# A decoder trunk's first k-tile in four transfers of 128 KB, and the first two tiles' terms alone at the beginning

## The chip, the core and the metric

The kernel runs on one core of a Trainium2 chip. The metric is the device time of one execution in microseconds (us), the median of several runs. A profile is one further execution, recorded by the hardware; its times are in us from the start of its span.

## The reference

Two layers of a causal decoder on 256 tokens of width 1024. Each layer has an attention and an MLP with squared ReLU, each followed by a layer norm of `alpha * x + f(x)`. Only its first product matters here: `x @ w_qkv` of the first attention (16 heads of 64), whose q and k columns are rotated and scored.

```
qkv = (x @ w_qkv).reshape(B, S, 3, H, dh)
q = apply_rotary(qkv[:, :, 0], cos, sin) * (dh ** -0.5)
k = apply_rotary(qkv[:, :, 1], cos, sin)
...
h = layer_norm(DEEPNORM_ALPHA * h + mix, ln_mix_g[i], ln_mix_b[i])
h = layer_norm(DEEPNORM_ALPHA * h + sq_relu_mlp(h, mlp_w_in[i], mlp_w_out[i]), ln_mlp_g[i], ln_mlp_b[i])
```

## The kernel before

**Products in three terms.** Every float32 operand of a large product is split into two fp32r parts, hi (a rounded copy) and lo (the rest), and a product is the sum of hi x hi, hi x lo and lo x hi. `split` (L349) makes them: hi on ScalarE (L351) or, where a part is marked for it, on VectorE as a cast (L353); lo always on VectorE as a subtraction (L356). All matmuls are issued through `mm` (L360).

**The first product.** x transposed stands in HBM beside the first six weight tiles (`NFIRST`), 128 columns each: `xw0` has, for each of eight k-tiles of 128 rows, 256 columns of x and 6 x 128 columns of weights, 1024 float32 columns or 512 KB. One k-tile is one object of the class `Stage` (L379). `STAGE_PARTS` says for k-tile 0, 1, 2 and all later ones how the six weight tiles are cut into parts for the splits, which engine makes each part's hi, and which parts go in one transfer on which queue: part 0 is x, and `(0, 1, "SP")` loads parts 0 to 1 through SP's queue. A part's split waits for the transfer that holds it. In the kernel before, k-tile 0 comes in two transfers: x and tile 0 (192 KB) on SP's queue, tiles 1 to 5 (320 KB) on ACT's. K-tile 1 has x and tiles 0 and 1 on SP's queue, the rest on ACT's; all later loads of the kernel are on SP's queue.

`Stage.mms` (L418) issues one matmul of 256 columns (the tokens) for one weight tile and one of the three terms; six tiles by three terms are the 18 matmuls of a k-tile. They accumulate in three PSUM banks (`acc`), two tiles in each:

```
start, stop = kt == term == j % 2 == 0, kt == KT - 1 and term == 2 and j % 2 == 1
op("PE", 0.12, lambda: mm(ps.t[:, j % 2 * S : j % 2 * S + S], w.t[:, c], xs[kt // 4].t[:, kt % 4, p, :], start, stop),
   [(w, (kt, self.part(j)))] + [(xs[kt // 4], (p, kt, m)) for m in range(2)], [ps])
```

**Fillers.** Ahead of the useful work TensorE runs fillers, matmuls of 512 columns on constants whose result nobody reads (`idle`, L451, one for each entry of `WARM`). One more filler, of 256 columns, stands behind the first useful matmul. In the profile they are written to `tp`, all useful ones of this stage to `acc`.

**What sets the order.** The kernel first collects all operations with estimated costs, then a planner (`Plan.order`) sorts them into one program order by due times, for all engines; buffers are handed out in that order. An engine runs its instructions in this order and waits on semaphores for its inputs. So an edit at one place can move instructions anywhere. DMA issues are instructions of SP or ACT; ACT's first instructions are two DMA issues, then a load of its function table, then the splits.

Of the kernel before, what the change touches and what calls it, by code (L numbers as in the profile page):

```python
# [47 lines left out]
NFIRST = 6  # L48
# [3 lines left out]


STAGE_PARTS = (
    ((1, 3, NFIRST), ("DVE", "ACT", "ACT"), ((0, 1, "SP"), (2, 3, "ACT"))),
    ((2, NFIRST), ("DVE", "ACT"), ((0, 1, "SP"), (2, 2, "ACT"))),
    ((2, NFIRST), ("ACT", "ACT"), ((0, 1, "SP"), (2, 2, "SP"))),
    ((NFIRST,), ("ACT",), ((0, 1, "SP"),)),
)
WARM = (512,) * 8  # L60

# [51 lines left out]
class Plan:  # L115
# [16 lines left out]
    def op(self, eng, cost, fn, reads=(), writes=(), xfer=0.0, early=0.0, ahead=0.0):  # L132
        o = Op()
        o.n, o.eng, o.cost, o.fn, o.xfer = len(self.ops), eng, cost, fn, xfer
        o.early, o.ahead = early, ahead
        o.preds, o.succs, o.bufs = set(), [], set()
        for group, is_write in ((reads, False), (writes, True)):
            for item in group:
                b, key = item if isinstance(item, tuple) else (item, None)
                o.bufs.add(b)  # L140
                for k, st in b.state.items():
                    if key is None or k is None or k == key:
                        if st[0] is not None:
                            o.preds.add(st[0])
                        if is_write:
                            o.preds.update(st[1])
                st = b.state.setdefault(key, [None, []])
                if is_write:
                    if key is None:
                        b.state = {None: [o, []]}  # L150
                    else:
                        st[0], st[1] = o, []
                else:
                    st[1].append(o)
        o.preds.discard(o)
        for p in o.preds:
            p.succs.append(o)
        for b in o.bufs:
            b.left += 1
        self.ops.append(o)  # L160
        return o
# [129 lines left out]
def tile_trunk(  # L291
# [37 lines left out]
    def mk(shape, dt, tag, bufs, space=None):  # L329
        uid[0] += 1  # L330
        return plan.buf(Bufs(space or sb, bufs), shape, dt, tag, bufs, f"{tag}_{uid[0]}")

    def psum(tag):
        return mk([P, 512], F32, tag, 4, ps_pool)
# [24 lines left out]
    def mm(out_ap, lhsT, rhs, start, stop):  # L359
        nc.tensor.matmul(out_ap, lhsT, rhs, start=start, stop=stop)  # L360
# [16 lines left out]
    xs = [mk([P, 4, 2, S], F32R, f"xs{i}", 1) for i in range(2)]  # L377
# [73 lines left out]
    def idle(n, reads=()):  # L451
        ones = nc.const_aps.tensor
        op(
            "PE", n / 2400, lambda: mm(idle_ps.t[:, :n], ones(1.0, [P, P], BF16), ones(1.0, [P, n], BF16), True, True),
            list(reads), [idle_ps],
        )

    for n in WARM:
        idle(n)
# [140 lines left out]

    first_ps = [psum("acc") for _ in range(NFIRST // 2)]
    for st in stages:
        for term in range(3):
            for j in range(NFIRST):
                st.mms(first_ps[j // 2], j, term)
                if st.kt == term == j == 0:
                    idle(256, [(st.hi, (0, 1)), (xs[0], (0, 0, 0))])


    turns = {"score": 0, "prob": 0}  # L610
# [680 lines left out]
```

## Time and profile before

| | |
|---|---|
| median of 3 runs | 559.83 us (559.78 to 559.93) |
| the profiled execution | 560.12 us |
| its span, first to last instruction | 558.3 us |
| TensorE busy | 550.3 us of the span, 3236 matmuls |
| VectorE, ScalarE busy | 412.1 us, 302.0 us |
| first useful matmul starts | 4.59 us |

In the profile PE is TensorE's matmul side, PEld its weight loads, DVE VectorE, ACT ScalarE, SP SyncE; SPq and ACTq are the issues of DMAs. A line such as `4.59 0.41 PE L360 MATMUL acc<-xs,whi ... x1 [0.25 <-ACT xs L351]` reads: start, duration, engine, line, operation, output and inputs by tile name, shapes, how many were merged into the row, and the idle time before with what ended it. A row that merges several has the time from the first one's start to the last one's end or their summed busy time, so neighbouring rows overlap. Matmuls are pipelined: the distance of two starts is less than the duration of one.

### The profile page before, as it was taken

What the parts mean: (1) busy time and instruction counts of PE and PEld (TensorE: products, weight loads), DVE (VectorE), ACT (ScalarE), POOL (GpSimd) and SP (SyncE); (2) the same over time, 40 slices, a digit from 0 to 9 for tenths busy, and PEclk for the clock granted to TensorE, in tenths of its full rate; (3) what the DMA queues carried; (4) which work ended last, traced back from release to release, by engine and by line L of the source; (5) the groups of instructions that cost most, each with busy time, mean ns of one, the idle gap of its engine ahead of it and who ended that gap; (6) DMA issues with size and microseconds to landing.
All of it is one profiled execution on the core that took longest, in us unless ns stands there. A gap on an engine that the chain in (4) does not pass through costs nothing.

```text
span 558.3 us, 8586 instructions
## 1 busy us (share of the span) xinstructions
PE 550.3 (99%) x3236; PEld 470.0 (84%) x3236; DVE 412.1 (74%) x726; ACT 302.0 (54%) x491; POOL 8.6 (2%) x13
## 2 busy tenths in 40 slices
PE   9999999999999999999999999999999999999995
PEld 7988888888888888888888889888888888888884
DVE  6799999897584764854879899789848548558446
ACT  6467898257555455455544566556654554555400
POOL 0000000000000000000000000010000000000001
PEclk9999999999999999999999999999999999999998
DMA  8985246548884754755437535526867456463001
GB/s 333 410 312 190 77 147 220 196 148 300 262 276 145 249 182 154 238 175 191 147 117 265 174 117 164 190 75 196 300 221 262 159 184 225 156 222 114 1 0 75
DMA packets 30136, 105.60 MB, mean 189 GB/s; under 512 B 3344, under 2 KB 4112, under 8 KB 30096
## 3 DMA queue, kind: packets, MB, share of 16 engines
q1 hardware_dynamic: 29808, 104.48, 54.6%
q8 instruction: 25, 0.41, 0.3%
q10 hardware_dynamic: 288, 0.59, 0.3%
q14 instruction: 15, 0.12, 0.1%
HBM read 104.01 MB, written 1.05 MB: 188 GB/s over the span
## 4 chain that ended last, share of the span: by engine, by line
PE 98%; DMA 1%; DVE 0%; POOLq 0%; DVEq 0%; ACT 0%; issue 0%
PE acc L360 59%; PE tp L360 36%; PE tp L689 3%; DMA raw<-in_xw_dram 1%; POOLq L1285 0%; DVE tok L556 0%; DVEq L1285 0%; DVE bst L823 0%; ACT xs L351 0%; DVE mv L801 0%; DVE rstd L802 0%; POOLq L804 0%
## 5 line engine op out<-in xcount | busy, mean ns | idle before, releaser
L356 DVE TENSOR_TENSOR wlo<-raw,whi 128x1024 fp32r<-128x1024 f32 (+3 forms) x186 | 218.2, 1192 | 100.4 <-PE tp L360 47.2
L351 ACT ACTIVATE whi<-raw 128x1024 fp32r<-128x1024 f32 (+1 forms) x184 | 189.0, 1042 | 113.5 <-PE acc L360 68.2
L360 PE MATMUL acc<-whi,ahi 128*128 128x512 f32 (+1 forms) x312 | 121.6, 390 | 0.0
L360 PE MATMUL acc<-wlo,ahi 128*128 128x512 f32 (+1 forms) x312 | 121.0, 388 | 0.0
L360 PE MATMUL tp<-xs,whi 128*128 128x512 f32 x448 | 104.6, 390 | 0.0
L360 PE MATMUL acc<-whi,alo 128*128 128x512 f32 (+1 forms) x312 | 102.7, 387 | 0.0
L360 PEld LDWEIGHTS tp<-xs,whi 128*128 128x128 f32 x448 | 84.0, 188 | 17.3
L360 PEld LDWEIGHTS acc<-whi,alo 128*128 128x128 f32 x312 | 58.6, 188 | 12.1
L360 PEld LDWEIGHTS acc<-whi,ahi 128*128 128x128 f32 x312 | 58.7, 188 | 11.5 <-issue 0.3
L360 PEld LDWEIGHTS acc<-wlo,ahi 128*128 128x128 f32 x312 | 58.7, 188 | 11.2
L360 PE MATMUL acc<-xs,whi 128*128 128x512 f32 (+1 forms) x272 | 56.8, 356 | 0.2 <-ACT xs L351 0.2
L360 PEld LDWEIGHTS tp<-xs,wlo 128*128 128x128 f32 x448 | 55.6, 192 | 1.1
L360 PE MATMUL tp<-xs,wlo 128*128 128x256 f32 x448 | 55.9, 283 | 0.0
L360 PEld LDWEIGHTS acc<-xs,whi 128*128 128x128 f32 x272 | 44.4, 189 | 8.0 <-ACT xs L351 1.2
L351 ACT ACTIVATE ahi<-ta 128x256 fp32r<-128x256 f32 x56 | 23.5, 419 | 44.5 <-DVE ta L556 44.3
L912 ACT ACTIVATE ta<-tp 128x256 f32<-128x256 f32 x56 | 21.3, 380 | 26.2 <-PE tp L360 26.2
L549 DVE TENSOR_TENSOR ta<-tp,ta 128x256 f32<-128x256 f32 x56 | 23.4, 419 | 12.7 <-ACT ta L912 12.6
L360 PE MATMUL acc<-xs,wlo 128*128 128x256 f32 x224 | 30.4, 283 | 0.0
L360 PEld LDWEIGHTS acc<-xs,wlo 128*128 128x128 f32 x224 | 29.1, 191 | 0.9
L360 PE MATMUL acc<-whi,xs 128*128 128x512 f32 (+1 forms) x112 | 29.1, 367 | 0.0
L360 PE MATMUL tp<-whi,xs 128*128 128x512 f32 x80 | 25.2, 396 | 0.0
L556 DVE SCALAR_TENSOR_TENSOR ta<-ta 128x256 f32<-128x256 f32 x56 | 23.8, 425 | 1.8
(102 smaller groups left out, 464.2 us busy)
## 6 DMA issues: line engine op xcount, KB each, us to landing
raw<-in_win_dram SPq DMA_DIRECT2D x64, 512.0 KB, 4.1
raw<-in_wout_dram SPq DMA_DIRECT2D x64, 512.0 KB, 3.9
raw<-in_wqk_dram SPq DMA_DIRECT2D x22, 512.0 KB, 5.5
raw<-in_wo_dram SPq DMA_DIRECT2D x14, 512.0 KB, 3.8
raw<-in_wv_dram SPq DMA_DIRECT2D x8, 512.0 KB, 5.4
g<-in_lng_dram SPq DMA_DIRECT2D x4, 512.0 KB, 7.0
b<-in_lnb_dram SPq DMA_DIRECT2D x4, 512.0 KB, 6.9
raw<-in_wv1a_dram SPq DMA_DIRECT2D x4, 512.0 KB, 3.9
```

Of the source, the lines that this page charges most:

```text
L351: op("ACT", act(n, sbuf=sbuf), lambda: nc.scalar.activation(hi(), src(), AF.Copy), r, whi)
L356: lambda: nc.vector.tensor_tensor(lo(), src(), f32(hi()), op=ALU.subtract), list(r) + list(whi), wlo,
L360: nc.tensor.matmul(out_ap, lhsT, rhs, start=start, stop=stop)
L549: op("DVE", dve(n) + extra, lambda: nc.vector.tensor_tensor(out_ap(), a(), b(), op=alu), r, w)
L556: lambda: nc.vector.scalar_tensor_tensor(dst(), a(), s(), b(), op0=o0, op1=o1), r, w,
L689: nc.tensor.transpose(ps.t[:, c : c + P], src(), ident.t)
L912: op("ACT", act(S), lambda: nc.scalar.activation(u(), ps.t[:, S:], AF.Copy), [ps], uk)
```

## The change

K-tile 0 comes in four transfers of 128 KB: x on SP's queue, tiles 0 and 1 on ACT's, tiles 2 and 3 on SP's, tiles 4 and 5 on ACT's. Its weight tiles are cut into three parts of two tiles (before: one, two and three); the first part's hi is made on VectorE, the others' on ScalarE, as before. Of k-tile 0's matmuls the three terms of tiles 0 and 1 are issued first, then the three terms of the other four; before, the order was by term over all six tiles. The filler among them stands behind the second useful matmul. One of the eight fillers ahead is gone.

```diff
 STAGE_PARTS = (
-    ((1, 3, NFIRST), ("DVE", "ACT", "ACT"), ((0, 1, "SP"), (2, 3, "ACT"))),
+    ((2, 4, NFIRST), ("DVE", "ACT", "ACT"), ((0, 0, "SP"), (1, 1, "ACT"), (2, 2, "SP"), (3, 3, "ACT"))),
     ((2, NFIRST), ("DVE", "ACT"), ((0, 1, "SP"), (2, 2, "ACT"))),
     ((2, NFIRST), ("ACT", "ACT"), ((0, 1, "SP"), (2, 2, "SP"))),
     ((NFIRST,), ("ACT",), ((0, 1, "SP"),)),
 )
-WARM = (512,) * 8
+WARM = (512,) * 7
...
     first_ps = [psum("acc") for _ in range(NFIRST // 2)]
     for st in stages:
-        for term in range(3):
-            for j in range(NFIRST):
-                st.mms(first_ps[j // 2], j, term)
-                if st.kt == term == j == 0:
-                    idle(256, [(st.hi, (0, 1)), (xs[0], (0, 0, 0))])
+
+        n = STAGE_PARTS[0][0][0]
+        todo = sorted((st.kt > 0 or j >= n, term, j) for term in range(3) for j in range(NFIRST))
+        for _, term, j in todo:
+            st.mms(first_ps[j // 2], j, term)
+            if st.kt == term == 0 and j == n - 1:
+                idle(256, [(st.hi, (0, 1)), (xs[0], (0, 0, 0))])
```

Built, the two programs differ only in the first instructions: on TensorE one filler less and the order of k-tile 0's 18 matmuls; on VectorE k-tile 0's cast has 256 columns and not 128, its three weight subtractions 256 each and not 128, 256 and 384, and x's lo stands ahead of all three and not behind the first; on ScalarE the two weight pieces have 256 columns each and not 256 and 384; on SP and ACT one DMA issue more each. From k-tile 1 on, every engine has the same instructions in the same order.

## The prediction

> **What bounds the kernel now.** I read the summary of the page first, then the chain that ended last.
>
> ```profile
> span 558.3 us, 8586 instructions
> ...
> PE 550.3 (99%) x3236; PEld 470.0 (84%) x3236; DVE 412.1 (74%) x726; ACT 302.0 (54%) x491; POOL 8.6 (2%) x13
> ...
> PE 98%; DMA 1%; DVE 0%; POOLq 0%; DVEq 0%; ACT 0%; issue 0%
> ```
>
> TensorE is busy for 550.3 of 558.3 us and carries 98% of the chain. So there are two ways to be faster: fewer TensorE slots, or a stretch in which TensorE has no useful work made shorter. The view of waits, for TensorE alone over the whole span, says where it stood still:
>
> ```profile
> PE tp L360 <- PEq L1276: 0.8, 1, 0.8
> PE acc L360 <- ACT xs L351: 0.2, 1, 0.2
> ```
>
> That is all: it starts at 0.8 us, waits 0.2 us for the first split of x, and then never idles by this view until its work is over. The chain at the beginning, and the timeline (the engines' rows that matter; start, length), show the stretch that the change edits:
>
> ```profile
> 0.73 3.37 DMA raw<-in_xw_dram
> 4.10 0.02 issue
> 4.12 0.42 ACT xs L351
> 4.55 0.04 issue
> 4.59 0.41 PE acc L360
> ...
> 5.13 22.93 PE acc L360 x175
> ```
>
> ```profile
> 0.73 0.89 ACTq L347 DMA_DIRECT2D raw<-in_xw_dram  x2
> 0.73 2.38 SPq L347 DMA_DIRECT2D raw<-in_xw_dram  x5
> ...
> 0.77 3.57 PE L360 MATMUL tp<-const-bfloat16-1.0 128*128 128x512 bf16 x8 [0.77 <-PEq L1276]
> ...
> 1.65 1.28 ACT L351 ACT_TABLE_LOAD   x1 [1.65 <-PEq L1276]
> ...
> 4.45 0.81 ACT L351 ACTIVATE whi<-raw 128x256 fp32r<-128x256 f32 x2
> ...
> 4.59 0.41 PE L360 MATMUL acc<-xs,whi 128*128 128x256 f32 x1 [0.25 <-ACT xs L351]
> 4.59 0.42 DVE L356 TENSOR_TENSOR xs<-raw,xs 128x256 fp32r<-128x256 f32 x1
> ...
> 4.84 0.28 PE L360 MATMUL tp<-const-bfloat16-1.0 128*128 128x256 bf16 x1
> ...
> 4.93 0.92 DVE L356 TENSOR_TENSOR wlo<-raw,whi 128x256 fp32r<-128x256 f32 x2
> 5.65 0.42 ACT L351 ACTIVATE xs<-raw 128x256 fp32r<-128x256 f32 x1 [0.39 <-DMA raw<-in_xw_dram]
> 5.77 0.29 DVE L353 CAST whi<-raw 128x256 fp32r<-128x256 f32 x1
> ...
> 6.10 0.43 DVE L356 TENSOR_TENSOR xs<-raw,xs 128x256 fp32r<-128x256 f32 x1
> ...
> 6.44 1.02 DVE L356 TENSOR_TENSOR wlo<-raw,whi 128x256 fp32r<-128x256 f32 x2
> 6.49 0.88 PE L360 MATMUL acc<-xs,wlo 128*128 128x256 f32 x6
> ...
> 7.21 0.64 PE L360 MATMUL acc<-xs,whi 128*128 128x256 f32 x4
> ```
>
> So the first useful matmul starts at 4.59: the first transfer lands at 4.10, ScalarE splits x in 0.42, and 0.05 goes to the signal. The 18 matmuls of the first k-tile and the small filler last from 4.59 to 7.21, 2.62 us. In steady state one of 256 columns takes a slot of (0.88 - 0.28) / 5 = 0.12, so 19 would take 2.28: some 0.34 is lost to the clock and to waits for ScalarE's second and third piece. All that the change can win lies ahead of 7.21. The order of the rest of every engine's instructions is unchanged.
>
> **The transfers.** Bytes over time (the last two columns are the DMA share and GB/s), then the two queues up to 3 us (q1 is SP's, q10 ACT's), then the first issues with their KB and the time to landing:
>
> ```profile
> 0.00:2.40 2.40, 1.63 (x4) 0.59 (x5) 0.09 (x2) 0.75 (x1) 0.76 (x5) 1.00 0.19 25
> 2.40:3.00 0.60, 0.60 (x3) 0.29 (x2) 0.00 (x0) 0.53 (x1) 0.00 (x0) 1.00 0.87 320
> 3.00:3.40 0.40, 0.40 (x3) 0.13 (x2) 0.00 (x0) 0.00 (x0) 0.00 (x0) 1.00 1.00 393
> 3.40:4.10 0.70, 0.70 (x3) 0.04 (x1) 0.00 (x0) 0.00 (x0) 0.00 (x0) 1.00 1.06 394
> ...
> 5.10:6.00 0.90, 0.90 (x8) 0.78 (x7) 0.90 (x3) 0.51 (x3) 0.00 (x0) 1.00 1.04 266
> 6.00:7.00 1.00, 1.00 (x11) 1.00 (x10) 0.96 (x4) 0.97 (x4) 0.00 (x0) 1.00 1.09 428
> ```
>
> ```profile
> q1 hardware_dynamic: 85, 0.13, 22.9%
> q10 hardware_dynamic: 47, 0.12, 10.1%
> ```
>
> ```profile
> raw<-in_xw_dram ACTq DMA_DIRECT2D x1, 320.0 KB, 3.6
> ...
> raw<-in_xw_dram SPq DMA_DIRECT2D x1, 192.0 KB, 3.4
> ```
>
> Summed up: 0.06 MB by 2.40, 0.25 by 3.00, 0.41 by 3.40, 0.69 by 4.10. By 3.00 the queues have moved 0.13 and 0.12 MB, so both are served side by side at about equal rates. SP's 192 KB (0.197 MB) are through when some 0.39 MB have moved in all, at 3.36; they are signalled at 4.10, a lag of 0.74. After the change x alone is first on SP's queue and two weight tiles on ACT's, 128 KB (0.131 MB) each. Both are through at 0.262 MB, at 3.03, and with the same lag they land at 3.77. Bounds: not at all earlier (4.10), if the lag belongs to the start of the stream and not to its bytes; and 3.65, from the other queue, whose 320 KB end the first k-tile at 0.73 + 3.6 = 4.33: half of that tile's 512 KB, at 394 GB/s, is 0.67 less. I take 3.75, next to the value from x's own queue.
>
> The Trainium skill (DMA: Bandwidth & Descriptors, "Issuing engines are not separate DMA queues") speaks against splitting: transfers issued from several engines run on the same 16 DMA engines and interleave, and only the issue time is saved. The two equal shares above agree; a queue of its own would then bring x nothing, and only the fewer bytes ahead of it count.
>
> Issues: SP and ACT each issue one more. ACT's cost 0.89 / 2 = 0.45, so the table load goes from 1.65 to 2.10 and ends at 3.38, ahead of 3.75: nothing as long as x lands after 3.38. SP's 2.38 / 5 = 0.48 moves its later issues from the second k-tile on; those transfers queue behind a saturated stream (about 390 GB/s), so that is hidden too.
>
> **TensorE's start.** With landing at 3.75 the first useful matmul starts at 3.75 + 0.47 (4.12 to 4.59 now) = 4.22. The groups of the first 8 us have the fillers' mean:
>
> ```profile
> L360 PE MATMUL tp<-const-bfloat16-1.0 128*128 128x512 bf16 x8 | 3.6, 628 | 0.8 <-PEq L1276 0.8
> ```
>
> Dropping one filler: eight end at 4.34, of mean 0.628, so the last starts at 3.71 and they are 0.42 apart; its slot would be over at 4.13, still ahead of 4.22; the seventh's is over at 3.71. The removal is worth 0 here and up to 0.09 with landing at 3.65, and matters only for landing ahead of 3.66. VectorE's first cast grows from one tile to two; the later cast of that size took 0.29, less than ScalarE's 0.42 beside it, so it sets nothing. No split is added: VectorE has a cast and three weight subtractions of 128 to 384 columns now and of 256 then, ScalarE two pieces, 640 columns in all now and 512 then.
>
> **The first k-tile.** The matmul at 4.59 took 0.41 and the filler at 4.84 took 0.28, while this group of equal width took 283 ns in the whole run:
>
> ```profile
> L360 PE MATMUL tp<-xs,wlo 128*128 128x256 f32 x448 | 55.9, 283 | 0.0
> ```
>
> So the clock opens between 4.59 and 4.84, which the granted-clock column does not show. Then, from 4.22: the first matmul's slot 0.25 (4.59 to 4.84), the second 0.21 (half a filler's slot, half its columns), the filler to 4.84; hi x lo of tiles 0 and 1 needs VectorE's lo of x, 4.22 + 0.42 + 0.05 = 4.69, so it starts at 4.84 and ends at 5.08. Their lo parts: VectorE starts them 0.34 after x's lo (4.59 to 4.93), a 256-wide one takes 0.42: 4.22 + 0.34 + 0.42 + 0.05 = 5.03, ready. Two slots, 5.32. The other twelve need ScalarE's two pieces of 256 columns: their transfers complete the 512 KB at some 4.33, and 0.81 gives 5.14 for both. Twelve slots of 0.12: 6.76. Against 7.21 that is 0.45 won: 0.37 from the start, 0.08 from waits that now have other tiles' terms in front.
>
> **The second k-tile.** Its x now stands behind 256 KB on SP's queue, not 192; in equal shares 0.131 MB more in all pass ahead of it, 0.31 us at 428 GB/s, 0.49 at 266. Nothing, if the queues take turns by packets and the longer rows had already had more than their half. So x lands at 5.65, 5.95 or 6.14. TensorE needs its hi at 6.76, its lo at 7.00 and the lo of tiles 0 and 1 at 7.24. VectorE's row: cast at landing + 0.12, x's lo 0.33 later, the next 0.34 later, for 0.42, and 0.05: landing + 1.26. That is 6.91, 7.21 or 7.40: no wait for the first two, 0.16 lost at the last. I take 0.03 lost, near the middle. From the third k-tile on, as many bytes as before stand in front.
>
> **Is it kept to the end?** Later stages:
>
> ```profile
> 24.00:40.00 16.00, 16.00 (x120) 13.47 (x119) 15.11 (x26) 8.89 (x15) 0.00 (x0) 1.00 0.90 349
> 40.00:100.00 60.00, 60.00 (x480) 50.70 (x479) 57.88 (x154) 48.97 (x118) 0.00 (x0) 1.00 0.49 167
> ```
>
> VectorE (third of the engines) is busy for 57.88 of 60 us in the attention stage, yet TensorE never waits. Its inputs there come from TensorE's own results, so they come as much earlier; loss between 0 and all 0.42, taken at 0.
>
> **Sum.** 0.45 - 0.03 = 0.42 us. The profiled execution took 560.12 (span 558.3 and 1.8 around it), 0.29 above the median of the runs, 559.83. So 559.70 for such an execution, 559.4 as median. 0.2% is 1.12 us, about what a measurement of this kernel can tell from no change, and this gain is 0.08%: smaller than that.
>
> **Rivals.**
> - No earlier landing, or the gain eaten by the second k-tile or by VectorE: 559.6 to 559.9. For it speaks that of the 3.37 us to landing 1.67 pass before 2.40 with 0.06 MB moved, a fixed part that fewer bytes do not shorten.
> - Slower: the clock opens late. Useful matmuls now follow a shorter run of fillers; the array stands idle from 3.71 to 4.22, as against 4.13 to 4.59, so 0.51 and not 0.46. If that breaks the count, full speed comes another 4.0 us (0.77 to 4.59-4.84) after the new start, at about 8.2. From 4.22 to 8.2 at 0.21 a slot TensorE does 18 matmuls and the filler; the present order has done 18 by 7.21 and eight more by 8.2: 8 x 0.12 = 0.96 behind, 560.8. It decides as soon as the idle stretch is over what the clock allows; with landing at 4.10 that is 0.88, full speed comes at 8.6 and 11.6 x 0.12 = 1.4 are missing, 561.2. Against it: the idle stretch is hardly longer. The Trainium skill (TensorE: Matmul & The Clock Gate, "What's actually happening") has a free-running window of 3.4 us; the next would open at about 8.1, the same price. Run to run it would scatter; 559.78 to 559.93 speaks against that.
> - More than forecast: landing at 3.65 or earlier, as the fillers now allow, 559.1 to 559.2.
>
> **How the numbers follow.** The forecast's mechanism 0.64, with 559.2 to 559.6; no gain 0.16; clock late 0.12; more 0.08. The range 559.0 to 560.0 takes in the first, the second and the last, 559.1 to 559.9, with 0.1 on each side for the scatter of the runs (559.78 to 559.93), and leaves out the clock's rival. Slower by over 0.2% (above 560.95) needs the late clock with late landing, or a price I do not see: 0.09. Faster by over 0.2% (below 558.71) would take a first matmul ahead of the fillers' end: 0.04. Within: 0.87.
>
> **What would show it.** Right: the first split of x at 3.65 to 3.9, the first useful matmul at 4.1 to 4.4, the second k-tile's first at 6.6 to 6.9, the same distance at 28 us and at the end. Wrong: a first split at 4.0 or later; 256-column matmuls still taking 0.41 after 5 us; a new row of TensorE waiting for VectorE near 7 us.

## The result and the profile after

The changed kernel takes 561.39 us (median of 14 runs, 560.48 to 562.17), the kernel before in the same session 560.03 (14 runs, 559.78 to 560.77): a ratio of 1.0022, 95% interval 1.0015 to 1.0029. It is slower by 0.22%, where 0.4 us less was forecast. The profiled execution took 561.6 with a span of 559.7; that of before, 560.12 and 558.3.

The page of the changed kernel: span, busy time, the chain by engine.

```profile
span 559.7 us, 8588 instructions
...
PE 550.7 (98%) x3235; PEld 470.3 (84%) x3235; DVE 412.2 (74%) x726; ACT 302.2 (54%) x491; POOL 8.6 (2%) x13
...
PE 97%; DMA 1%; DVE 0%; POOLq 0%; SPq 0%; DVEq 0%; ACT 0%; issue 0%
```

TensorE is busy for 0.4 us more and the span is 1.4 longer, so about 1.0 us is new idle time. The view of waits, TensorE alone, names it:

```profile
PE acc L360 <- ACT xs L351: 1.2, 1, 1.2
PE tp L360 <- PEq L1278: 0.8, 1, 0.8
```

It is the row that was 0.2 us before. The timeline of TensorE, then of ScalarE and VectorE, tells that it now stands at another place:

```profile
0.77 3.15 PE L360 MATMUL tp<-const-bfloat16-1.0 128*128 128x512 bf16 x7 [0.77 <-PEq L1278]
3.93 0.76 PE L360 MATMUL acc<-xs,whi 128*128 128x256 f32 x2
4.50 0.44 PE L360 MATMUL tp<-const-bfloat16-1.0 128*128 128x256 bf16 x1
...
5.14 0.40 PE L360 MATMUL acc<-xs,wlo 128*128 128x256 f32 x2
5.37 1.12 PE L360 MATMUL acc<-xs,whi 128*128 128x256 f32 x8
6.33 0.64 PE L360 MATMUL acc<-xs,wlo 128*128 128x256 f32 x4
8.12 0.96 PE L360 MATMUL acc<-xs,whi 128*128 128x256 f32 x4 [1.16 <-ACT xs L351]
8.93 0.50 PE L360 MATMUL acc<-xs,wlo 128*128 128x256 f32 x2
9.26 1.11 PE L360 MATMUL acc<-xs,whi 128*128 128x256 f32 x8
```

```profile
2.13 1.28 ACT L351 ACT_TABLE_LOAD   x1 [2.13 <-issue]
3.43 0.42 ACT L351 ACTIVATE xs<-raw 128x256 fp32r<-128x256 f32 x1
...
7.66 0.42 ACT L351 ACTIVATE xs<-raw 128x256 fp32r<-128x256 f32 x1 [2.64 <-DMA raw<-in_xw_dram]
```

```profile
3.49 0.29 DVE L353 CAST whi<-raw 128x256 fp32r<-128x256 f32 x1 [2.60 <-DMA raw<-in_xw_dram]
...
8.11 0.43 DVE L356 TENSOR_TENSOR xs<-raw,xs 128x256 fp32r<-128x256 f32 x1 [0.15 <-ACT xs L351]
8.45 1.02 DVE L356 TENSOR_TENSOR wlo<-raw,whi 128x256 fp32r<-128x256 f32 x2
```

The same eight matmuls of the second k-tile stood here before:

```profile
7.92 1.12 PE L360 MATMUL acc<-xs,whi 128*128 128x256 f32 x8
```

The first k-tile is better than before: first useful matmul at 3.93 (before 4.59), its last slot over at about 6.81 (before 7.21). Then the second k-tile's x is split at 7.66, where before it was 5.65; TensorE stands still for 1.16 us and starts the second k-tile at 8.12 in place of 7.21. Its first matmuls then follow VectorE step by step (x's lo done at 8.11 + 0.43, the first tiles' lo at 8.93), so that the eight that began at 7.92 now begin at 9.26: 1.34 us late, which is nearly all of the span's 1.4. Nothing behind it gives any of it back.

The transfers, in half microseconds (the last two columns are the DMA engines' busy share and GB/s), after; below it one row of before for 3.0 to 6.5 us:

```profile
3.00:3.50 0.50, 0.50 (x3) 0.01 (x1) 0.01 (x1) 0.49 (x2) 0.00 (x0) 1.00 0.87 291
...
4.50:5.00 0.50, 0.50 (x4) 0.50 (x4) 0.40 (x2) 0.50 (x2) 0.00 (x0) 1.00 0.97 307
5.00:5.50 0.50, 0.50 (x6) 0.50 (x6) 0.50 (x2) 0.01 (x1) 0.00 (x0) 1.00 1.17 225
5.50:6.00 0.50, 0.50 (x7) 0.50 (x6) 0.00 (x0) 0.00 (x0) 0.00 (x0) 1.00 0.77 201
6.00:6.50 0.50, 0.50 (x7) 0.50 (x6) 0.00 (x0) 0.00 (x0) 0.00 (x0) 1.00 0.72 258
```

```profile
3.00:6.50 3.50, 3.25 (x18) 1.92 (x17) 2.30 (x8) 1.99 (x5) 0.00 (x0) 1.00 1.04 358
```

After, the same window has 277 GB/s. In 3.5 us that is 0.28 MB less, more than half of a k-tile. The busy share must be read with care: the view books a packet's whole time to the row in which it starts, so 1.17, 0.77 and 0.72 belong together. Spread over the time that each packet took, the packets in the trace keep the engines busy for 0.73, 0.94 and 1.00 of these three rows. So engines are empty for a part of the time, and for another part they are busy and move little.

Single packets tell more. Most of those of 2 KB take 84 ns in both kernels. Of the packets that start between 2.4 and 6.5 us the longest took 366 ns before; after, five that start between 5.46 and 5.66 took 636 to 1172 ns. A transfer raises its semaphore 16 times in the trace, as many times as there are DMA engines (the trace does not name the engine; each signal is read here as one engine's share), and a split waits for the last. For the transfer with the second k-tile's x the 16 signals came between 4.93 and 5.62 before. After, 14 had come by 5.72, and the last two came at 7.12 and 7.63; by 6.98 nine shares of the transfer behind it, the third k-tile's first, were already in. So in this execution most of that x was there on time and TensorE stood still for the last two shares.

### The profile page after: what moved, and what is told of

The parts are those of the page before. It is cut to its first block, busy times and chain, and to the rows that moved or that the text cites. A ratio compares the mean times of both kernels' runs of the same rounds, so it can differ in the third digit from the quotient of the medians.

```text
span 559.7 us, 8588 instructions
## 1 busy us (share of the span) xinstructions
PE 550.7 (98%) x3235; PEld 470.3 (84%) x3235; DVE 412.2 (74%) x726; ACT 302.2 (54%) x491; POOL 8.6 (2%) x13
## 4 chain that ended last, share of the span: by engine, by line
PE 97%; DMA 1%; DVE 0%; POOLq 0%; SPq 0%; DVEq 0%; ACT 0%; issue 0%
PE acc L360 58%; PE tp L360 36%; PE tp L691 3%; DMA raw<-in_xw_dram 1%; POOLq L1287 0%; DVE tok L556 0%; SPq L347 0%; DVEq L1287 0%; DVE bst L825 0%; ACT xs L351 0%; DVE mv L803 0%; DVE rstd L804 0%; POOLq L806 0%
## 5 line engine op out<-in xcount | busy, mean ns | idle before, releaser
L356 DVE TENSOR_TENSOR wlo<-raw,whi 128x1024 fp32r<-128x1024 f32 (+2 forms) x186 | 218.1, 1191 | 99.0 <-PE tp L360 52.8
```

Source lines behind the costliest of these rows:

```text
L356: lambda: nc.vector.tensor_tensor(lo(), src(), f32(hi()), op=ALU.subtract), list(r) + list(whi), wlo,
```

## The experiments

Each kernel is the changed kernel, or the kernel before where it says so, with the edit shown; instructions behind the first k-tiles keep their order. Theory A: the four short transfers of the first k-tile delay the second. Theory B: its two halves, side by side on both queues, delay each other. Theory C: the fillers or the order of terms did it, by the clock or otherwise. The later letters are explained where they come. One profiled execution of each in a table: the first k-tile's transfers in KB (SP's queue / ACT's), the start of ScalarE's first split of x, the mean GB/s from 3.0 to 6.5 us, the start of its splits of the second k-tile's x and last four tiles, the first useful matmul; then the median of the runs (us). Most kernels have ten or eleven runs, before and after 14, hold_g 8, loads_only 7, before_four 6, before_three and four_by_rows 4.

| kernel | first k-tile | x split | GB/s | second k-tile | first matmul | median |
|---|---|---|---|---|---|---|
| before_one | 512 / none | 4.94 | 396 | 5.98, 6.29 | 5.41 | 562.45 |
| before | 192 / 320 | 4.12 | 358 | 5.65, 5.97 | 4.59 | 560.03 |
| two_equal | 256 / 256 | 3.92 | 349 | 5.41, 5.73 | 4.39 | 560.07 |
| two_equal_w8 | 256 / 256 | 4.08 | 338 | 5.94, 6.26 | 4.55 | 560.14 |
| two_by_1k | 256 / 256, rows 1 KB | 4.17 | 330 | 5.61, 7.88 | 5.20 | 561.51 |
| merged | 2x128 / 2x128 | 3.37 | 320 | 6.50, 6.83 | 3.97 | 561.55 |
| before_three | 192 / 128, 192 | 3.75 | 299 | 6.12, 7.77 | 4.22 | 562.12 |
| all_sp_merged | 4x128 / none | 3.12 | 294 | 7.58, 7.90 | 4.06 | 561.16 |
| after | 2x128 / 2x128 | 3.43 | 277 | 7.66, 7.98 | 3.93 | 561.39 |
| hold_kt3 | 2x128 / 2x128 | 3.44 | 272 | 7.74, 8.06 | 4.07 | 560.71 |
| kt1_one_queue | 2x128 / 2x128 | 3.36 | 264 | 5.41, 7.90 | 3.97 | 560.56 |
| two_sp | 2x256 / none | 3.42 | 259 | 5.54, 6.88 | 3.89 | 560.54 |
| four_by_rows | 2x128 / 2x128, 64 rows | 5.32 | 251 | 7.05, 7.38 | 5.79 | 563.36 |
| two_sp_merged | 2x256 / none | 3.38 | 249 | 7.57, 7.89 | 3.84 | 561.08 |
| warm8 | 2x128 / 2x128 | 3.44 | 247 | 7.75, 8.32 | 3.96 | 561.51 |
| packed | 2x128 / 2x128 | 3.43 | 247 | 7.56, 7.88 | 3.98 | 561.53 |
| all_sp | 4x128 / none | 3.19 | 245 | 6.05, 8.05 | 4.05 | 561.34 |
| before_four | 128, 64 / 128, 192 | 3.44 | 239 | 7.82, 8.14 | 4.15 | 561.75 |
| hold_g | 2x128 / 2x128 | 3.43 | 236 | 7.56, 7.88 | 4.04 | 561.30 |
| loads_only | 2x128 / 2x128 | 3.43 | 214 | 7.64, 7.96 | 4.03 | 561.36 |

**The transfers alone, and the fillers alone.** loads_only keeps the four transfers, and the parts that go with them, but has the order of terms and the eight fillers of before; warm8 has only the eighth filler back.

```
loads_only: todo = [(term, j) for term in range(3) for j in range(NFIRST)], idle(256) after the first matmul
loads_only, warm8: WARM = (512,) * 8
```

> The changed kernel's transfers and parts, but the matmuls ordered by term over all six tiles and eight fillers, as in the kernel before. Theory A (the transfers alone do the harm: the second k-tile's land at about 8 and not at 5.6, and TensorE stands still for it): a wait of about 1 us for the second k-tile again, 561.2 to 561.7. Theory C (the shorter run of fillers or the new order of the matmuls does it, through TensorE's clock): 559.5 to 560.1, no wait before the second k-tile.

> The changed kernel with eight fillers ahead as before. Theory C (the filler's absence costs the time): back to 559.5 to 560.1. Theories A and B (it lies in the transfers): the first useful matmul 0.2 later than in the changed kernel, at 4.15, the wait for the second k-tile as long less 0.2, the time as the changed kernel's within 0.2, 561.2 to 561.6.

loads_only: ratio 1.0023 (1.0012 to 1.0034); warm8: 1.0021 (1.0011 to 1.0030). TensorE's wait is there in both; that of loads_only:

```profile
PE acc L360 <- ACT xs L351: 1.0, 1, 1.0
```

So the transfers with their parts cost all of it, and theory C falls; that it is the transfers and not the parts, the next kernel shows, which keeps the parts.

**Two equal transfers.**

```
-((0, 0, "SP"), (1, 1, "ACT"), (2, 2, "SP"), (3, 3, "ACT"))
+((0, 1, "SP"), (2, 3, "ACT"))       # two_equal; two_equal_w8: and WARM = (512,) * 8
```

> The changed kernel with the first k-tile in two transfers of 256 KB: x and tiles 0 and 1 on SP's queue, tiles 2 to 5 on ACT's. Seven fillers and the new order of matmuls stay. Theory A (four small transfers do it): the second k-tile lands at 5.5 to 6.0, first k-tile's x at 4.0 to 4.2, 559.7 to 560.2. Theory B (both queues side by side on equal halves of the same rows do it, whatever the number of transfers): the second k-tile at 7 or later, over 561. Theory C: as the changed kernel, 561.4.

> The two equal transfers of 256 KB with eight fillers in place of seven. Theory G (the runs of 561.6 to 561.9 with seven fillers were a clock that opened one window late, as in the profiled one, since the fillers ended before the first useful matmul): no run over 560.8, the slots of the profiled run at full clock from about 5 us, median 559.7 to 560.1. Rival (the late runs come from late transfers): some runs still over 561.3.

two_equal: ratio 1.0009 (0.9999 to 1.0019); seven runs at 559.82 to 560.51 and three at 561.59 to 561.89. The second k-tile is on time (5.41), so the delay is gone with the two extra transfers. The profile fell on one of the three late runs (561.76), and its TensorE rows show why:

```profile
4.39 0.80 PE L360 MATMUL acc<-xs,whi 128*128 128x256 f32 x2 [0.47 <-ACT xs L351]
...
6.08 1.91 PE L360 MATMUL acc<-xs,whi 128*128 128x256 f32 x8
...
9.56 1.12 PE L360 MATMUL acc<-xs,whi 128*128 128x256 f32 x8
```

The same eight slots take 1.91 us at 6.08 and 1.12 at 9.56: the trace records the change to the full clock at 9.08 us (at 4.68 in before, 5.08 in after). TensorE had stood idle for 0.47 us ahead of its first useful matmul. Theory G (the clock one window late) said that an eighth filler would cure this, and the runs agree: two_equal_w8 waits 0.2 us there and has ten runs within 560.07 to 560.65, ratio 0.9999 (0.9989 to 1.0008). Three late runs of ten against none of ten support it but do not prove it; the kernel before, with 0.25 us of idle time, has one such run (562.21) among the 31 of one session.

**The second k-tile on one queue.** `Stage.load` sends the last four tiles of the second k-tile through SP's queue.

> The changed kernel, but the second k-tile's last four weight tiles are loaded through SP's queue, behind its x and first two tiles, not through ACT's. Theory B (the second k-tile is late because both queues move its halves side by side): its x lands at 5.2 to 6.0 and the kernel gains what was forecast, 559.3 to 559.9. Theory A (what stands ahead, the four small transfers, does it): x still lands at 7 or later, 561 to 561.7.

Ratio 1.0009 (0.9999 to 1.0018). Theory B falls in part: x is split at 5.41 as it said, against theory A's sign (7 or later), but the stall then hits the four tiles behind it (7.90):

```profile
PE acc L360 <- ACT whi L351: 1.0, 1, 1.0
```

So the lateness does not need two halves side by side on both queues: here all of the second k-tile is on SP's queue, and the tiles behind x are late.

**Short rows, number, or place in memory.** Theory D: the number of transfers; E: rows of 1024 B, so twice the packets; F: short pieces 4096 B apart in memory.

```
four_by_rows: partitions 0-63 on SP, 64-127 on ACT; columns 0-511, then 512-1023     # 4 transfers, rows of 2 KB
two_by_1k:    SP moves x and tiles 2, 3 in one, ACT tiles 0, 1 and 4, 5; WARM x8      # 2 transfers, rows of 1 KB
packed:       xw0[0] stored part by part, each of 128 KB in one piece
```

> The first k-tile in four transfers of 128 KB as in the changed kernel, on the same queues and at the same places, but cut by rows: each moves 64 partitions with rows of 2048 B (x with tiles 0 and 1 first, by its halves on both queues), in place of 128 partitions with rows of 1024 B. So 256 rows in place of 512. Theory D (the number of transfers on the queues delays what comes behind them): the second k-tile is as late as in the changed kernel, TensorE waits about 1 us for it, time 561.2 to 561.6. Theory E (the rows of 1024 B, twice as many for the same bytes, delay it): second k-tile's x has landed by 6.2 us, wait under 0.4 us, time 559.5 to 560.3. Theory F (it is the stride of the short pieces in memory): as E, or half way.

> The first k-tile in two transfers of 256 KB, but of rows of 1024 B: SP's moves x and tiles 2, 3, ACT's tiles 0, 1 and 4, 5, so 512 rows as in the changed kernel with half its transfers (and eight fillers). x and the tiles all land near 4.2 us, the first useful matmul is at 4.5 to 4.7. Theory D (number of transfers): no delay of the second k-tile beyond 0.4 us, time 559.8 to 560.4. Theory E (rows of 1024 B): its x is split after 7 us, TensorE waits over 0.5 us for it, time 561.0 to 561.8.

> The changed kernel with the first k-tile's four parts each stored as one piece of 128 KB in memory; transfers, queues, rows in the SBUF (1024 B) and all that follows are the same. Theory F (short pieces 4096 B apart in memory are read slowly): the wait of about 1 us for the second k-tile goes, time 559.5 to 560.2. Theories D and E: no change, 561.2 to 561.6.

packed: 1.0018 (1.0008 to 1.0027), wait and landing as in after, so F falls. two_by_1k: 1.0022 (1.0012 to 1.0033), but not by theory E's mechanism: the rate is 330, the second k-tile's x is split at 5.61, and only its last four tiles are late (7.88), behind a first k-tile that is late itself. (These tiles are nearly as late as in after, 7.98.) Its cost is the late first matmul (5.20, tiles 0 and 1 landed late) and, by the two groups of its runs, the clock: five runs at 560.37 to 560.83, five at 562.18 to 562.55. The profile is of the first group. four_by_rows, 1.0056 (1.0041 to 1.0071), is spoiled as a time: ScalarE's table load came to stand behind a wait for x (4.03 to 5.31), so x was split at 5.32. Its transfers still say something. Half microseconds again:

```profile
3.50:4.00 0.50, 0.42 (x1) 0.00 (x0) 0.00 (x0) 0.00 (x0) 0.00 (x0) 1.00 1.34 201
4.00:4.50 0.50, 0.00 (x0) 0.00 (x0) 0.29 (x1) 0.47 (x1) 0.00 (x0) 1.00 0.73 107
```

Rows of 2 KB, and the rate falls to 201 and 107; at 3.5 to 4.0 neither ScalarE nor VectorE has done anything yet, so the splits that x lets loose don't cause it here. Four transfers with long rows lose the rate, two with short rows keep most of it: for D, against E, as far as one profile of each goes. The four are also cut by partitions, which no other kernel is, and short rows have their own late tiles, so E is weakened and not excluded.

**What is issued later.** Theory H: SP's issues from 3.5 us on, which x's landing lets loose, disturb what is under way. GpSimd copies one column of the second k-tile's x into the buffer of the fourth (hold_kt3) or fifth (hold_g) k-tile, so that this transfer and all after it are issued only then.

```
+nc.gpsimd.tensor_copy(dst()[:, 0:1], stages[1].raw.t[:, 0:1])     # ahead of that k-tile's dma_start
```

> The changed kernel with one more small operation: GpSimd copies one column of the second k-tile's x, as soon as it has landed, into the buffer of the fourth k-tile, so that SP issues the fourth k-tile and all that follows only then (before, SP issues it at 3.49 us, as soon as the first x has landed). Theory H (transfers issued from 3.5 us on, while the second k-tile is under way, slow it): the second k-tile's x is split by 6.2 us, TensorE's wait of about 1 us for it goes, time 559.4 to 560.2. Theory D (the number of transfers ahead of it is enough): it is split after 7 us as before, time 561.2 to 562.

> The same hold one transfer later: the fourth k-tile is issued at about 3.5 us as in the changed kernel, the fifth and all that follow only when the second k-tile's x has landed. Theory H: if the fifth and sixth k-tile's issues (3.86 and 4.50 us) do the harm, 559.4 to 560.2; if the fourth's does, 561.2 to 561.8 as the changed kernel. Theory D: 561.2 to 561.8.

hold_kt3: 560.71 (560.16 to 561.75), 1.0012 (1.0002 to 1.0021); hold_g: 1.0024 (1.0014 to 1.0034). The profile of hold_kt3: SP's issues, ScalarE, GpSimd.

```profile
0.74 7.69 SPq L351 DMA_DIRECT2D raw<-in_xw_dram  x6
```

```profile
7.74 0.42 ACT L357 ACTIVATE xs<-raw 128x256 fp32r<-128x256 f32 x1 [2.36 <-DMA raw<-in_xw_dram]
```

```profile
7.77 0.30 POOL L350 COPY raw<-raw 128x1 f32<-128x1 f32 x1 [6.24 <-DMA raw<-in_xw_dram]
```

SP's sixth transfer, the fourth k-tile, waits for the copy at 7.77, and the second k-tile was as late as ever: H falls as the cause for all that is issued from the fourth k-tile on. The third k-tile's two transfers are still issued before. The median is 0.7 us below that of after in another session; whether the hold helps some runs a little is open.

**More transfers, or fewer, in the kernel before.** ACT's 320 KB as 128 + 192 (before_three); SP's 192 KB as 128 + 64 besides (before_four); all 512 KB in one transfer on SP's queue (before_one). Nothing else differs from the kernel before.

```
+for c in cuts: queue.dma_start(dst()[:, c], src[:, c])
```

> The kernel before with ACT's first transfer of 320 KB (tiles 1 to 5) issued as two, of 128 KB (rows of 1024 B) and 192 KB (rows of 1536 B); everything else, its order of terms and its fillers too, is the kernel before. x lands at 4.1 us as before. Theory D (each transfer ahead delays the second k-tile): its x is split 0.3 to 0.8 us later than the 5.65 of before, which lies within TensorE's slack of about 1.2 us: time 559.9 to 560.6. Theory H (it is what is issued from 3.5 us on, which x's landing lets loose): as before, 559.8 to 560.2.

> The kernel before with both transfers of the first k-tile issued as two: x 128 KB and the first weight tile 64 KB on SP's queue, 128 KB and 192 KB on ACT's; everything else is the kernel before. Theory D: the second k-tile's x is split after 7 us and TensorE waits about 0.5 to 1 us for it, time 560.8 to 561.8. Theory H: x lands earlier than in the kernel before and lets the next issues loose about 0.6 us earlier, so the harm is that of the changed kernel or less, 560.4 to 561.6. Theory E (short rows): as Theory D, somewhat less.

> The kernel before with the first k-tile in a single transfer of 512 KB on SP's queue (two in the kernel before); ACT's queue begins with the second k-tile's part. x lands with the last weights, at 4.2 to 4.8 us by 512 KB at 250 to 400 GB/s, beside the second k-tile's ACT part. Theory D: no stretch of 0.5 us under 300 GB/s before 6 us, the second k-tile's x by 5.6 us; time 559.9 to 560.6 by the later x. If the stretch of low rate at 5 to 6 us of the kernel before stays as it is, the number of transfers isn't what sets it.

before_three: 562.12, ratio 1.0038 (1.0023 to 1.0053, four runs); before_four: 1.0029 (1.0017 to 1.0041); before_one: 1.0032 (1.0019 to 1.0045). One transfer more is enough to spoil the kernel before: the last 192 KB, split at 5.69, then held TensorE for 1.24 us within the first k-tile:

```profile
6.26 1.79 PE L365 MATMUL acc<-xs,whi 128*128 128x256 f32 x9 [1.24 <-ACT whi L356]
7.85 1.48 PE L365 MATMUL acc<-xs,wlo 128*128 128x256 f32 x6
```

Its profile (562.7, the slowest of the four runs) has a second loss: six slots take 1.48 and not 0.88, since by the trace the clock, full from 3.48 on, was at half from 6.89 to 10.31. With a single transfer the weak stretch of the kernel before (225 GB/s at 5.5 to 6.0) is gone (a row of before, then one of before_one):

```profile
5.50:6.00 0.50, 0.50 (x5) 0.50 (x5) 0.50 (x2) 0.35 (x2) 0.00 (x0) 1.00 0.87 225
```

```profile
3.00:6.50 3.50, 2.08 (x11) 1.11 (x10) 1.53 (x5) 1.56 (x5) 0.00 (x0) 1.00 1.03 396
```

It is slower for another reason: x now lands with the last weights, the first matmul comes at 5.41, after 1.4 us of idle time, and seven of its ten runs (562.28 to 563.08 against 560.76 to 561.15) bear the mark of a late clock. The profile (560.76) is one of the other three: there the clock was full from 3.49 on.

**Number in all, or two queues.** merged moves the second and third k-tile by one transfer of 512 KB each; all_sp puts all six first transfers on SP's queue (theory J: two queues side by side disturb each other); all_sp_merged does both. Then, with two transfers of 256 KB for the first k-tile on SP's queue and eight fillers: two_sp, and two_sp_merged, with as few transfers up to the third k-tile as any kernel here (four).

```
VIA, WHOLE = None, (1, 2)     # merged        VIA, WHOLE = "SP", ()      # all_sp, two_sp
VIA, WHOLE = "SP", (1, 2)     # all_sp_merged, two_sp_merged
```

> The changed kernel with the second and the third k-tile each moved by one transfer of 512 KB on SP's queue in place of two of 256 KB: six transfers up to the third k-tile as in the kernel before (2, 2, 2 there, 4, 1, 1 here), the first k-tile's four unchanged. Theory D in its form that the number in all counts: the second k-tile is split by 6.5 us, TensorE waits under 0.3 us for it, time 559.5 to 560.3. Theory D in its form that the first k-tile's own four transfers do it: it is split after 7.4 us, time 561.2 to 562.2.

> The changed kernel with all four transfers of the first and both of the second k-tile on SP's queue, none on ACT's, so that they run one after another in place of side by side. Theory J (two queues side by side with short transfers disturb each other): x has landed by 3.3 us, no stretch of 0.5 us under 280 GB/s before 6 us, the second k-tile split by 6.2 us, time 559.0 to 560.0. Theory D (the number of transfers, on whichever queue): it is split after 7 us, 561 to 562.

> Both together: everything on SP's queue, the first k-tile in four transfers, the second and third in one of 512 KB each. Theory J: as all_sp. Theory D in its form of the number in all: the second k-tile by 6.5 us, 559.3 to 560.3. Theory D by the first k-tile's own four: after 7 us, 561 to 562.

> The changed kernel with two transfers of 256 KB for the first k-tile (x and tiles 0, 1, then tiles 2 to 5), then one of 512 KB each for the second and third, all in order on SP's queue, and eight fillers. Where short transfers one behind another ran on SP's queue alone, x and the next 128 KB had landed at 3.6 us. Theory D (the number of transfers): x and tiles 0, 1 by 3.7 us, the first useful matmul at 4.2 to 4.4, no stretch of 0.5 us under 300 GB/s from 3 us on, the second k-tile split before 6.8 us: time 559.5 to 560.0. Rival (the single queue starts too slowly, at 230 to 280 GB/s up to 4 us, so that x comes no sooner than the 4.1 us of before): 559.9 to 560.6.

> The same with the second and third k-tile in two transfers of 256 KB each, all on SP's queue. Theory D with the number in all: slower than the one with merged transfers, the second k-tile's later part split 0.3 to 1 us later, time 559.9 to 560.8. Theory D with the first k-tile's alone: the same time as the merged one, within 0.3 us.

merged: 1.0018 (1.0007 to 1.0029), two runs at 560.26 and 560.31, the profiled one among them (second k-tile at 6.50), the other eight at 560.98 to 562.09. all_sp: 1.0015 (1.0005 to 1.0025); all_sp_merged: 1.0015 (1.0005 to 1.0024): J falls (in all_sp x is split at 6.05 as it said, but the four tiles behind it at 8.05). two_sp_merged: 1.0014 (1.0005 to 1.0023). It had four transfers, x at 3.38, and then the deepest hole of all:

```profile
3.00:3.50 0.50, 0.50 (x3) 0.16 (x2) 0.12 (x1) 0.12 (x1) 0.00 (x0) 1.00 1.47 303
3.50:4.00 0.50, 0.50 (x3) 0.16 (x1) 0.35 (x2) 0.29 (x1) 0.00 (x0) 1.00 0.72 61
4.00:4.50 0.50, 0.50 (x3) 0.47 (x2) 0.50 (x2) 0.00 (x0) 0.00 (x0) 1.00 1.33 172
```

So the number of transfers, the last form of theory D, isn't the cause by itself either. two_sp: 560.54 (559.51 to 561.21), 1.0003 (0.9994 to 1.0012); with two transfers more than two_sp_merged it is 0.5 us faster, against theory D's sign. Its profile has no wait of TensorE but the one for its start,

```profile
PE tp L361 <- PEq L1281: 0.8, 1, 0.8
```

yet its span is 558.6, 0.3 longer than that of before, although its first useful matmul came 0.70 earlier. The rows show why:

```profile
5.66 1.50 PE L361 MATMUL acc<-xs,whi 128*128 128x256 f32 x8
7.00 0.64 PE L361 MATMUL acc<-xs,wlo 128*128 128x256 f32 x4
```

The eight slots at 5.66 take 1.50 and not 1.12, and the first k-tile is over at 7.48 (before 7.21): by the trace the clock was full only from 6.53 on. So here the transfers held, and the clock took the gain. Its two lowest runs, 559.51 and 559.60, lie 0.28 and 0.19 below the lowest of before in that session (559.79); no profile shows what they had that the others lacked. No version beat the kernel before.

**What stays open.** The table can be read as two groups, though each row is one execution and only 10 GB/s lie between them. The kernels whose first transfers are one of 512 KB, or two of 192 KB and more on the two queues, keep 330 to 396 GB/s from 3.0 to 6.5 us. All others, which have 128 KB transfers, a third transfer, or two of 256 KB in line on one queue, have 214 to 320 (merged's 320 is from one of its two fast runs). The longest packet that starts between 2.4 and 6.5 us parts them in the same way: 0.31 to 0.50 us in the first group, 0.59 to 1.88 in the others. In all but one of these ScalarE could split x by 3.75; in the first group it was 3.92 at the earliest. So what goes with the loss is that a first piece is through early and the next pieces start early; that this causes it is not shown. Nor is the pattern of the lateness always that of after: in loads_only eight of the 16 shares of the second k-tile's x were signalled by 5.85 and the other eight from 7.26 to 7.62. Why single packets then take a microsecond and engines stand empty, the runs don't settle. Not the cause by themselves are the fillers and the order of terms, the distance of the pieces in memory, issues from the fourth k-tile on, the second queue, and the number of transfers in all; against the splits and the short rows there is less evidence.

## Why the prediction was wrong, step by step

**Landing of x, 3.75: right in sign, too cautious.** VectorE began to cast the tiles beside it at 3.49, and the last of the 16 signals of x's transfer came at 3.31. The bounds reached down to 3.65 only; 0.26 MB had moved by about 2.9 us, so the lag behind the bytes was some 0.4 and not the fixed 0.74 that the steps took.

**ACT's extra issue: right, with its condition gone.** Table load forecast 2.10 to 3.38, measured 2.13 to 3.41. "Nothing as long as x lands after 3.38" no longer held: ScalarE split x straight from the table load. In kt1_one_queue and merged, where ACT issues one transfer less, the split waited for x and came at 3.36 and 3.37, so the issue costs x 0.07 us at most.

**First useful matmul, 4.22: 3.93.** The step of 0.47 from landing to matmul held (0.50).

**First k-tile done at 6.76: about 6.81.** The clock opened at 5.08 by the trace, not at 4.59 to 4.84 (the filler at 4.50 still took 0.44, the eight slots at 5.37 took 1.12), which took back the 0.29 of the earlier start. The gain of 0.40 was there, 0.45 forecast.

**The second k-tile: the step that failed.** It took the stream behind the first k-tile as given: x late by 0, 0.31 or 0.49 us, by the extra bytes ahead of it at 428 and 266 GB/s, a cost of 0.03 and at most 0.16; and "those transfers queue behind a saturated stream (about 390 GB/s), so that is hidden too". ScalarE split that x at 7.66 in place of 5.65, 2.0 us later. The stream was no longer saturated (201 to 258 GB/s at 5.0 to 6.5), and its shares no longer came together: 14 of the 16 were signalled by 5.72, within the forecast's 5.65 to 6.14, but a transfer has landed only with its last share, and that came at 7.63. The steps had counted bytes at a mean rate and had no term for shares that come in apart. loads_only and two_equal show that the four transfers did it; why they did is open. The chain behind it was right: the start of the split + 1.26 gives 8.92 for the first tiles' lo, TensorE used it at 8.93. So the term of the sum that was 0.03 is 1.7 us (the second k-tile's eight begin 1.34 late although the first was done 0.40 early), and 0.42 won became 1.3 lost. The row of 266 GB/s at 5.1 to 6.0 in the kernel before was a warning: the stream already had a weak stretch, and it was read as a constant of the place, not as something that the cut of the transfers can change (before_one, with a single one, has 381 GB/s or more there).

**Kept to the end: right,** for the loss: VectorE is busy for 57.87 of 60 us at 40 to 100 us, as before, and the later stages changed little of it: 1.34 us at the second k-tile's eight, 1.4 in the span.

**The rivals.** The late clock wasn't it in the profiled execution: the clock opened at 5.08, not at 8.2, and TensorE never waits between its fillers and the first useful matmul. But a late clock does occur: with 0.47 us of idle time the profile of two_equal has it (9.08), and three of its ten runs lie 1.6 us above the others (560.8 to 561.2 was the forecast time, 561.6 to 561.9 the measured). That the first three runs of before lay within 559.78 to 559.93 spoke against scatter less than it seemed to: 31 later ones of the same kernel reach from 559.79 to 562.21. The remark of the Trainium skill (DMA: Bandwidth & Descriptors, "Issuing engines are not separate DMA queues") is that transfers issued from several engines run on the same DMA engines and that only the time to issue them is saved. No gain came here, which agrees; it names no loss, and no run shows that interleaving is what cost it, since one queue did no better (1.0015). Of its signs of being right, the first split (3.43 for 3.65 to 3.9) and the first useful matmul (3.93 for 4.1 to 4.4) came earlier than forecast, the second k-tile's first matmul (8.12 for 6.6 to 6.9) much later. None of the signs that were to show the prediction wrong was the right one: it expected a wait for VectorE near 7 us, and the wait is for ScalarE's split, behind the transfer.

## What to carry to other kernels

A transfer that arrives earlier is worth only what the next ones leave of it: when the first piece is cut smaller, follow the bytes of the second and third piece too, with a price for a slower stream and not only for the bytes ahead. A rate that has a dip in the kernel before isn't a saturated stream, and the dip is no bound for another cut: 266 GB/s was the forecast's own lower bound, and it gave 0.16 us where 1.7 were lost. Look at the last of a transfer's 16 signals, not at the mean rate. And a gain of 0.4 us at the start of a kernel has to be seen through the clock's scatter: when the fillers ahead of the first useful matmul are trimmed, keep the idle stretch in front of it short; with half a microsecond three runs of ten were 1.6 us longer here.

## What the runs showed of the hardware

- The 16 DMA engines' rate in the first microseconds depends on how the first 512 KB are cut: 396 GB/s from 3.0 to 6.5 us with one transfer, 330 to 358 with two on two queues, 249 and 259 with two in line on one queue, 214 to 320 with four of 128 KB, down to 61 in one half microsecond (one profile each). From 8.0 to 8.5 us it is 406 in after and 426 in before.
- Two ways of losing it: busy engines that move little (0.72 busy for 61 GB/s at 3.5 to 4.0 in two_sp_merged, where the kernel before moved 394 at 1.06 from 3.4 to 4.1) and empty engines (0.41 busy for 147 GB/s at 4.5 to 5.0 in loads_only). A packet of 2 KB that mostly takes 84 ns took up to 1172 in after.
- A transfer signals 16 times, and the signals can lie far apart: within 0.69 us for the second k-tile's x in before, over 2.96 us in after (4.67 to 7.63).
- TensorE's clock opens at different times in kernels whose fillers all start at 0.77 or 0.78 us: between 3.43 (packed) and 6.69 (before_four) in 18 of the 20 profiles, at 9.08 in two_equal (0.47 us idle ahead of the first useful matmul) and at 9.71 in four_by_rows (1.87). It can also be lost again: in before_three, after an idle stretch of 1.24 us, it was at half from 6.89 to 10.31. Idle time alone does not decide it: two_by_1k (1.23) and before_one (1.42) had the full clock from 3.46 and 3.49 on in their profiles and kept it.
- Run times that fall in two groups some 1.5 us apart suggest the same without a profile: with 0.2 us of idle time no late run of ten (two_equal_w8), with 0.5 three (two_equal), 1.2 five (two_by_1k), 1.4 seven (before_one).
